# Five engine queues of a hybrid decoder step: orders by the scheduler and a partial table, replaced by whole tables

## The chip, the cores and the metric

The kernel runs on one core of a Trainium2 chip. The metric is the device time of one execution in microseconds (us). The kernel before took 2063.24 us (median of 3 runs, 2061.25 to 2066.89). A core has five engines, each with a queue of instructions that it works through in order: TensorE (PE, matrix products; PEld is its weight loading), VectorE (DVE), ScalarE (ACT), GpSimd (POOL) and SyncE (SP, which here issues most of the DMA transfers). Engines wait for each other through semaphores. The order in which a queue holds its instructions is fixed when the program is built.

## The reference, cut to what matters

One layer of a hybrid decoder for a prompt of 2048 tokens and 8 single decode tokens, in fp32, with a model width of 1024:

```python
xn = _rmsnorm(x, norm1_g)
z = jnp.einsum('btd,de->bte', xn, w_in)            # 1792 columns: RG-LRU x | gate | q | k | v
xr, gr, q, k, v = jnp.split(z, IN_SPLITS, axis=-1)
xc, new_conv = _causal_conv(xr, conv_buf, conv_w, conv_b)
hs, h_last = _rglru(xc, h0, ...)                    # gated linear recurrence over the tokens
rec = hs * jax.nn.gelu(gr)
att, ... = sliding-window attention (8 heads of 64, 2 KV heads, window 128, a sink per head)
mix = jnp.concatenate([_rmsnorm(rec, rec_norm_g), _rmsnorm(att, attn_norm_g)], axis=-1)
h = x + jnp.einsum('bte,ed->btd', mix, w_out)
hn = _rmsnorm(h, norm2_g)
ff = jax.nn.silu(hn @ w_gate) * (hn @ w_up)         # 2816 wide
y = h + ff @ w_down
```

Then a final RMSNorm. The outputs are y, the last 128 K and V rows, the conv history and the recurrent state, for prompt and decode tokens.

## The kernel before, in words

**Products.** Each fp32 matrix is split into a high and a low part, and each product is made of three matmuls (high by high, high by low, low by high), so that one 128x128 block of weights over 8 blocks of the contraction takes 24 matmuls.

**First half (up to about 690 us).** The 2056 tokens are cut into four sub-blocks (s = 0 to 3, 520 + 3 x 512). For each, the input projection makes 14 column units (products ip{s}_{u}); the units feed conv, gates (products g{s}_{c}) and scan of the recurrent branch on VectorE and ScalarE (`rec_chunk`, `gate_chunk`), and attention items of 128 queries and one KV head (`attn_item`): scores s, a softmax, transposes pt, their copies to SBUF as high part `pth` (ScalarE, L984) and low part `ptl` (VectorE, L985), products o with V, and the addition into `ratt` (L997). Group norms (`group_norm`, with small products st_ for sums and bc_ for broadcasting; rc is the recurrent group, at the attention group) lead to the output projection (products op{s}_{m}; `out_unit`, and `out_half` for the last sub-block), whose result is added to the residual `xres` and stored to `hs` in device memory.

**Second half.** The feed-forward part works on three token groups gi = 0, 1, 2 of two halves each (344 or 342 columns) and 11 pairs p of weight blocks. Gate and up products of a pair are done by a seven-product scheme for 2x2 blocks (keys g{gi}_{p}_{r} and u{gi}_{p}_{r}; `products`). It needs mixed inputs: `hn_mix` loads rows of `hs` (tiles n, L517; scaled on VectorE, L521; added, L529) and stores sums to `mixed`; `hn_load` loads them and splits them into hn. Weight sums are made from loads rg, ru and rd on ScalarE, VectorE and GpSimd (L1224, L1225, L1259, L1294, L1326). VectorE adds the products from PSUM into c_g and c_u (L1410); ScalarE copies some (L1431 to L1438) and applies SiLU (L1389). The down projection runs on the high and low parts fh, fl (L1380, L1381) either plainly (`down`, products pd, VectorE adds into y at L1469) or in the seven-product way (`down_parts`, products pw, adds at L1500). The final norm of the last group is `finish_last`: f21 is the second half of group 2, which ends first, and f20 the first half; each has sums (st_f), a root and a reciprocal (L1558, L1559), a broadcast product (bc_f), eight scalings (L1577; for f20 two on GpSimd, L1575) and eight stores.

**What sets the order.** Each step of work is a generator that is handed to `Chains`, which runs generators by time and sets a priority for the scheduler that then makes each engine's queue. `at` and `ahead` move the priority of single instructions. On top stand hand-made orders, as dependencies that hold two instructions of one engine in order and need no semaphore: `PE_ORDER`, a table of TensorE's products by key and count from the start into the first pair of the feed-forward part; `AFTER`, seven pairs on VectorE and ScalarE; `FIRST_DVE` for the first sub-block's splits; `keep`, which holds some loads and products in program order; and, for the end, `F_PLACE`, `F_HOLD` with the lists `tail_pd`, `tail_add`, `ends`, `held`. The rest, TensorE's order from then on included, is the scheduler's.

**Fillings.** `filled` puts matmuls of a block of ones into a PSUM tile before its first real product, as many as `FILLS` counts under the key w_ and the tile's name:

```python
for _ in range(FILLS["w_" + name]):
```

There are 75 of them, each 128x256: 17 before the first sums (w_st_x0), 13 before w_st_at0, 13 before w_op3_0_0, 20 in eight small groups (5 w_g1_2_0_0, 4 w_pt2_0_0, 4 w_ps_u0_0_2, 2 w_pt15_0_0, 2 w_op3_3_1, one each of w_bc_x1_0, w_o8_0, w_bc_rc3_0), and at the end 9 w_st_f2_0 and 3 w_bc_f2_0.

Of the kernel before, what the change touches and what calls it, by code (L numbers as in the profile page):

```python
# [59 lines left out]
F_PLACE = [3, 6]  # L60
F_HOLD = [2, 5]
# [19 lines left out]
def plan():  # L81
# [34 lines left out]
ip0_1_1:3 ip0_12_0 ip0_1_0:2 ip0_1_1:2 ip0_12_0 ip0_1_0 ip0_1_1 ip0_12_0:4 ip0_12_1:6 ip0_1_0:3 ip0_1_1:3 ip0_12_0:3
ip0_1_0:2 ip0_1_1:2 ip0_12_0:2 ip0_12_1:5 ip0_9_0:5 st_x0:5 ip0_9_0:9 ip0_9_1:24 ip0_9_0:10 bc_x0_0:4 ip0_8_0:24
ip0_8_1:4 bc_x0_4 ip0_8_1:20 ip0_0_0:24 ip0_0_1:23 g0_1_0_0 ip0_0_1 ip0_3_0:24 g0_1_0_260 ip0_3_1:17 g0_1_1_0
ip0_3_1:7 ip0_11_0:18 g0_1_1_260 ip0_11_0:6 ip0_11_1:15 vt0_0 ip0_11_1:9 ip0_10_0:23 vt0_1 ip0_10_0 ip0_10_1:24
ip0_13_0:10 vt0_2 ip0_13_0:14 ip0_13_1:6 vt0_3 ip0_13_1:18 ip0_2_0:7 s0_0_0:4 ip0_2_0:5 g0_0_0_0 s0_0_1:4 ip0_2_0:12  # L120
ip0_2_1:6 s0_1_0:4 s0_1_1:4 ip0_2_1:2 g0_0_0_260 ip0_2_1:13 pt0_0_1:4 ip0_2_1 s1_0_0:4 ip0_2_1:2 ip0_5_0:3 s1_0_1:4
ip0_5_0 g0_0_1_0 ip0_5_0:9 o0_0_0 ip0_5_0:11 ip0_5_1 s1_1_0:4 ip0_5_1:2 pt0_1_1:4 o0_0_0 ip0_5_1:4 g0_0_1_260
ip0_5_1:12 s1_1_1:2 o0_1_0 s1_1_1:2 ip0_5_1:5 ip0_4_0:6 s2_0_0:4 ip0_4_0:3 o0_1_0 ip0_4_0:11 pt1_0_0:4 ip0_4_0:2
s2_0_1:4 ip0_4_0:2 ip0_4_1:24 ip1_8_0:15 ip0_6_0:2 o1_0_0 ip0_6_0:8 pt1_0_1 o1_0_0 pt1_0_1:3 ip0_6_0 ip1_8_0
g0_3_0_0 ip0_6_0:13 ip0_6_1 ip1_8_0:2 ip0_6_1:15 o1_0_1 g0_3_0_260 s2_1_0:4 ip0_6_1 ip1_8_0 ip0_6_1 pt1_1_0
ip0_6_1:5 o1_0_1 s2_1_1:4 pt1_1_0:3 ip0_6_1 ip1_8_0:5 ip1_9_0 g0_3_1_0 ip1_9_0:19 ip0_7_0:9 ip1_9_0:2 pt1_1_1 o1_1_0
pt1_1_1:3 g0_3_1_260 ip1_9_0:2 ip0_7_0:2 o1_1_0 ip0_7_0:13 w_bc_x1_0 bc_x1_0 s3_0_0:3 s3_0_1:4 ip0_7_1 s3_0_0
ip0_7_1 o1_1_1:2 bc_x1_0 w_pt2_0_0:4 ip0_7_1 bc_x1_0 ip0_7_1 bc_x1_0 ip0_7_1:2 pt2_0_0:4 ip0_7_1:18 ip1_10_0:2
o2_0_0:2 pt2_0_1:3 g0_2_0_0 ip1_10_0:12 pt2_0_1 ip1_10_0:10 ip1_11_0:2 o2_0_1 ip1_11_0 s3_1_0:4 pt2_1_0:4 g0_2_0_260
ip1_11_0 s3_1_1:4 ip1_11_0:2 o2_0_1 ip1_11_0:11 g0_2_1_0 pt2_1_1:3 ip1_11_0:7 ip1_4_0:4 o2_1_0 ip1_4_0 pt2_1_1  # L130
ip1_4_0 o2_1_0 g0_2_1_260 ip1_4_0:18 ip1_0_0:2 o2_1_1 ip1_0_0 vt1_0 ip1_0_0:6 dS:2 o2_1_1 pt3_0_0:4 ip1_0_0:5 dS:6
ip1_0_0:6 o3_0_0 ip1_0_0:4 ip1_12_0:2 dS2:2 ip1_12_0:2 pt3_0_1 o3_0_0 ip1_12_0:2 pt3_0_1:3 ip1_12_0:18 ip1_13_0:6
o3_0_1 ip1_13_0:2 o3_0_1 ip1_13_0:3 pt3_1_0:4 ip1_13_0:9 dS3 ip1_13_0 dS3 ip1_13_0:3 ip1_1_0:8 pt3_1_1:2 o3_1_0
pt3_1_1 ip1_1_0:2 pt3_1_1 o3_1_0 dS4:4 s4_0_0 ip1_1_0:2 o3_1_1 s4_0_1:3 s4_0_0:3 s4_0_1 dS4:4 ip1_1_0 o3_1_1
ip1_1_0:11 ip1_5_0:6 dS5:2 s4_1_0:2 s4_1_1:4 ip1_5_0 vt1_1 ip1_5_0:3 s4_1_0:2 ip1_5_0:8 pt4_0_0:2 ip1_5_0 pt4_0_0:2
ip1_5_0:5 ip1_2_0:2 s5_0_0:4 ip1_2_0 s5_0_1:4 ip1_2_0 vt1_2 ip1_2_0:8 o4_0_0 ip1_2_0:6 pt4_0_1 o4_0_0 pt4_0_1:3
ip1_2_0:3 vt1_3 ip1_2_0:3 o4_0_1 s5_1_0:4 s5_1_1:4 o4_0_1 st_rc0 pt4_1_0:4 st_rc0:4 ip1_6_0:15 pt4_1_1:4 bc_rc0_0:3
s6_0_0:4 bc_rc0_0 s6_0_1 ip1_6_0:4 s6_0_1:3 pt5_0_0 bc_rc0_4 pt5_0_0:3 g1_0_0_0 g1_0_1_0 w_st_at0:13 ip1_6_0
st_at0:5 ip1_6_0:4 ip1_3_0:24 ip1_7_0:3 bc_at0_0:4 ip1_7_0:18 bc_at0_4 ip1_7_0:3 op0_0_0:12 op0_0_260:8 g1_1_0_0
op0_0_260:4 op0_1_0:12 op0_0_0 op0_0_260 op0_1_0 op0_0_260:2 op0_0_0:3 op0_1_0:6 op0_0_0:6 op0_1_0:3 op0_0_260:9  # L140
g1_1_1_0 op0_0_0:2 op0_1_0:2 o4_1_0:2 op0_1_260:4 o4_1_1:2 op0_1_260:20 op0_2_0:11 pt5_0_1:4 o5_0_0:2 op0_2_0:13
op0_2_260:13 s6_1_0:3 s6_1_1:4 s6_1_0 op0_2_260:4 o5_0_1 op0_2_260:7 op0_3_0 w_g1_2_0_0:5 g1_2_0_0 pt5_1_0
op0_3_0:12 o5_0_1 op0_3_0:2 pt5_1_0:3 op0_3_0:9 op0_3_260:17 g1_2_1_0 op0_3_260:7 op0_4_0:24 op0_4_260:6 pt5_1_1:4
op0_4_260:2 o5_1_0:2 op0_4_260:16 op0_5_0 o5_1_1 op0_5_0:11 s7_0_0:4 op0_5_0:3 o5_1_1 op0_5_0:4 s7_0_1:4 pt6_0_0:2
# [24 lines left out]
ip3_4_0:2 ip3_1_0:2 g3_0_0_0 ip3_1_0:2 s13_0_0 pt12_0_0 o11_1_1 pt12_0_0 ip3_1_0 pt12_0_0:2 ip3_1_0:5 s13_0_0:3
# [1560 lines left out]
```

## Time and profile before

| | |
|---|---|
| median of 3 runs | 2063.24 us (2061.25 to 2066.89) |
| profiled execution, first to last instruction | 2054.6 us |
| median of the runs less that span | 8.6 us |
| TensorE busy | 2015.9 us (98%) |
| weight loading busy | 1908.1 us (93%) |
| VectorE busy | 1459.9 us (71%) |
| ScalarE busy | 944.6 us (46%) |
| GpSimd busy | 906.5 us (44%) |
| granted TensorE clock, mean | 0.997 |

The span is that of one execution taken by the hardware profiler; its own time outside the span is not recorded, so its distance to the median of the runs stands in the table. In rows of groups, the columns are: source line, engine, operation, output and inputs by tile names, shape, count; busy time and mean duration in ns; idle time of the engine just before, and what ended it. In rows of windows: stretch, length, busy time and count of PE, PEld, DVE, ACT and POOL, granted clock (1.00 is full), DMA share and GB/s. In rows of a timeline: start, duration, engine, line, operation, tiles, shapes, count, and in brackets the idle time before with its releaser. In rows of waits: engine, operation and line that waited, what ended the wait; sum, times, longest, in us.

### The profile page before, as it was taken

Reading aid. Unit: us, or ns where it says so; the run is one execution under the profiler, and the core shown is the slowest. Engines: PE = TensorE matmul, PEld = TensorE weight load, DVE = VectorE, ACT = ScalarE, POOL = GpSimd, SP = SyncE. Lnnn points to the kernel's source line nnn. Section 1 sums busy time; section 2 is a strip of 40 time slices with the busy share of each in tenths; the row PEclk is TensorE's granted clock in tenths of the full one; section 3 lists DMA queues with packets and bytes.
Section 4 is the critical chain, followed back from the end, with each engine's and each line's share of the span. In section 5 each row is a group of like instructions: output and inputs, shape, how many; then the busy total and the mean of one; then the engine's idle time right before and its main releaser. Section 6 shows DMA issues by size and latency. Waiting matters only on the chain.

```text
span 2054.6 us, 34857 instructions
## 1 busy us (share of the span) xinstructions
PE 2015.9 (98%) x12319; PEld 1908.1 (93%) x12319; DVE 1459.9 (71%) x2694; ACT 944.6 (46%) x1960; POOL 906.5 (44%) x799
## 2 busy tenths in 40 slices
PE   9999999999999999999999999999999999999998
PEld 9988787878777899999999999999999999999998
DVE  6877886767985766666654667777768666777675
ACT  6764774553664543343334533333335433433343
POOL 5311342020122787567656645556457522322333
PEclk9999999999999999999999999999999999999999
DMA  9864584576688856666546677776677675566652
GB/s 329 293 213 143 188 275 159 175 233 210 208 261 280 314 200 223 205 210 207 207 172 210 229 260 258 227 229 221 222 253 265 211 251 189 183 197 196 197 179 96
DMA packets 208991, 450.98 MB, mean 219 GB/s; under 512 B 25232, under 2 KB 82720, under 8 KB 208800
## 3 DMA queue, kind: packets, MB, share of 16 engines
q1 hardware_dynamic: 205184, 445.73, 65.2%
q10 hardware_dynamic: 3632, 3.02, 0.4%
q8 instruction: 97, 1.59, 0.3%
q14 instruction: 78, 0.64, 0.1%
HBM read 335.89 MB, written 113.84 MB: 219 GB/s over the span
## 4 chain that ended last, share of the span: by engine, by line
PE 77%; DVE 9%; DMA 6%; ACT 3%; issue 2%; POOL 1%; SPq 0%; DVEq 0%; ACTq 0%; POOLq 0%
PE ps_u L396 19%; PE ps_g L396 19%; PE pw L396 11%; PE pd L396 10%; PE ip L396 10%; PE op L396 4%; DMA n<-hs 3%; DMA xs<-in_xT 1%; DMA m<-mixed 1%; PE o L396 1%; PE pt L401 1%; DVE sc L974 1%; DVE sc L963 1%; PE s L396 1%; DMA mixed<-n 1%
## 5 line engine op out<-in xcount | busy, mean ns | idle before, releaser
L396 PE MATMUL ps_g<-hn,w_g 128*128 128x342 f32 (+1 forms) x2772 | 489.4, 320 | 4.6 <-DVE c_u L1410 1.8
L396 PE MATMUL ps_u<-hn,w_u 128*128 128x342 f32 (+1 forms) x2772 | 479.9, 319 | 1.9 <-ACT c_u L1436 1.3
L396 PEld LDWEIGHTS ps_g<-hn,w_g 128*128 128x128 f32 x2772 | 445.1, 188 | 6.0 <-DVE c_u L1410 2.3
L396 PEld LDWEIGHTS ps_u<-hn,w_u 128*128 128x128 f32 x2772 | 444.2, 188 | 2.6 <-ACT c_u L1436 1.6
L396 PE MATMUL ip<-xn,w_in 128*128 128x512 f32 (+1 forms) x1680 | 353.4, 358 | 1.9 <-ACT xn L431 1.8
L396 PEld LDWEIGHTS ip<-xn,w_in 128*128 128x128 f32 x1680 | 270.1, 189 | 46.0 <-issue 3.8
L1500 DVE TENSOR_TENSOR y<-y,pw 128x342 f32<-128x342 f32 x504 | 238.7, 504 | 73.0 <-PE pw L396 72.2
L396 PE MATMUL pd<-fh,w_d 128*128 128x344 f32 (+1 forms) x960 | 239.4, 320 | 0.6 <-DVE y L1469 0.6
L396 PE MATMUL op<-mix,w_out 128*128 128x512 f32 (+1 forms) x960 | 203.4, 357 | 0.5 <-DVE rrec L763 0.3
L396 PEld LDWEIGHTS op<-mix,w_out 128*128 128x128 f32 x960 | 155.4, 188 | 29.3 <-issue 5.0
L1469 DVE TENSOR_TENSOR y<-y,pd 128x344 f32<-128x344 f32 (+1 forms) x240 | 117.9, 507 | 75.3 <-PE pd L396 70.7
L396 PEld LDWEIGHTS pd<-fh,w_d 128*128 128x128 f32 x960 | 168.3, 188 | 1.4 <-DVE y L1469 1.1
L396 PE MATMUL pw<-fh,wd 128*128 128x342 f32 x576 | 165.6, 319 | 1.2 <-DVE y L1500 1.2
L396 PE MATMUL pd<-fl,w_d 128*128 128x344 f32 (+1 forms) x480 | 153.4, 320 | 0.0
L1381 DVE TENSOR_TENSOR fl<-c_u,fh 128x342 fp32r<-128x342 f32 (+1 forms) x132 | 107.1, 815 | 48.3 <-ACT fh L1380 47.9
L1225 POOL TENSOR_TENSOR w_u<-ru,w_u 128x512 fp32r<-128x512 f32 x44 | 58.9, 1338 | 181.6 <-ACT w_u L1224 155.0
L1392 POOL TENSOR_TENSOR c_u<-c_u,c_g 128x342 f32<-128x342 f32 (+1 forms) x60 | 60.5, 1008 | 170.7 <-DVE c_u L1410 132.1
L1380 ACT CAST fh<-c_u 128x342 fp32r<-128x342 f32 (+1 forms) x132 | 63.0, 480 | 157.8 <-POOL c_u L1392 61.9
L396 PE MATMUL pw<-t,wd 128*128 128x342 f32 x648 | 126.7, 320 | 2.6 <-DVE t L1381 1.7
L1410 DVE TENSOR_TENSOR c_u<-c_u,ps_u 128x342 f32<-128x342 f32 (+1 forms) x99 | 50.2, 507 | 100.3 <-PE ps_u L396 100.1
L396 PEld LDWEIGHTS pw<-t,wd 128*128 128x128 f32 x648 | 106.0, 188 | 4.4 <-DVE t L1381 2.5
L396 PEld LDWEIGHTS pw<-fh,wd 128*128 128x128 f32 x576 | 105.3, 189 | 1.7 <-DVE y L1500 1.5
(316 smaller groups left out, 3507.4 us busy)
## 6 DMA issues: line engine op xcount, KB each, us to landing
w_g<-split_g SPq DMA_DIRECT2D x88, 512.0 KB, 4.2
w_u<-split_u SPq DMA_DIRECT2D x88, 512.0 KB, 4.9
w_in<-split_w SPq DMA_DIRECT2D x84, 512.0 KB, 3.5
rg<-in_wgate SPq DMA_DIRECT2D x110, 256.0 KB, 3.1
ru<-in_wup SPq DMA_DIRECT2D x110, 256.0 KB, 3.2
w_out<-split_w SPq DMA_DIRECT2D x48, 512.0 KB, 4.4
split_g<-w_g SPq DMA_DIRECT2D x44, 512.0 KB, 3.6
split_u<-w_u SPq DMA_DIRECT2D x44, 512.0 KB, 2.7
```

The lines of the kernel that those rows point to most:

```text
L396: r = nc.tensor.matmul(*args, **kw)
L401: r = nc.tensor.transpose(*args)
L963: seen[f"sm{gb}_{kv}_{g}"] = nc.vector.tensor_tensor_reduce(sc[:, g, :kn], ps[:, gi * 256:gi * 256 + kn], mask[:, k0:k0 + kn], -SCALE, ns[ ...
L974: nc.vector.tensor_scalar(sc[:, g, :kn], sc[:, g, :kn], mx[:, 1, g:g + 1], None, ALU.mult)
L1225: lo_eng.tensor_tensor(w[:, 1, :], src, w[:, 0, :].bitcast(F32), op=ALU.subtract)
L1380: nc.scalar.copy(hi, v)
L1381: nc.vector.tensor_tensor(lo, v, hi.bitcast(F32), ALU.subtract)
L1392: (nc.vector if p == NPAIR - 1 or src is not v else eng(E_MUL[2 * h + n])).tensor_tensor(v, src, g, op=ALU.mult)
L1410: nc.vector.tensor_tensor(o, a, b, op)
L1469: r = nc.vector.tensor_tensor(ys[gi, n, m], ys[gi, n, m], ps, ALU.add)
L1500: nc.vector.tensor_tensor(v, v, ps, ALU.add)
```

## The change

The orders of all five queues are now stated for the whole program, in a table `ORDER` with one text for each engine. An entry is a key, for ":n" instructions in a row, with "+k" taking the k-th of those that the key has left instead of the first. TensorE's keys are products as before; the other engines' keys are the generators, whose instructions `Chains` now records. `order` chains each queue by the same semaphore-free dependencies as before, and takes every instruction that a key has. `PE_ORDER`, `AFTER`, `FIRST_DVE`, `keep`, `F_PLACE`, `F_HOLD` and the lists of the tail are removed, and so are the fillings that the tables don't have: 46 of 75 go, 17 w_st_x0, 9 w_st_f2_0 and 3 w_bc_f2_0 stay. Tiles, buffers, transfers and arithmetic are as before, and so are the counts of instructions on the four other engines.

```diff
-AFTER = [
-    ("xl2_5", "xc1_2_3"), ("xt3_1", "pth5_1_1"),
...
-PE_ORDER = """
-w_st_x0:13 ip0_1_0 ip0_1_1 w_st_x0:4 ip0_12_0 ip0_12_1 ip0_1_0:2 ip0_1_1:2 ip0_12_0:2 ip0_12_1:2 ip0_1_0 ip0_1_1
...
-s6_0_0:4 bc_rc0_0 s6_0_1 ip1_6_0:4 s6_0_1:3 pt5_0_0 bc_rc0_4 pt5_0_0:3 g1_0_0_0 g1_0_1_0 w_st_at0:13 ip1_6_0
-st_at0:5 ip1_6_0:4 ip1_3_0:24 ip1_7_0:3 bc_at0_0:4 ip1_7_0:18 bc_at0_4 ip1_7_0:3 op0_0_0:12 op0_0_260:8 g1_1_0_0
...
-op0_3_0:12 o5_0_1 op0_3_0:2 pt5_1_0:3 op0_3_0:9 op0_3_260:17 g1_2_1_0 op0_3_260:7 op0_4_0:24 op0_4_260:6 pt5_1_1:4
-op0_4_260:2 o5_1_0:2 op0_4_260:16 op0_5_0 o5_1_1 op0_5_0:11 s7_0_0:4 op0_5_0:3 o5_1_1 op0_5_0:4 s7_0_1:4 pt6_0_0:2
...
+ORDER = {
+    "PE": """
+w_st_x0:17 ip0_1_0 ip0_1_1 ip0_12_1 ip0_12_0 ip0_1_0:2 ip0_1_1:2 ip0_1_0 ip0_12_1 ip0_1_1 ip0_12_0:2 ip0_12_1 ip0_12_0
...
+s5_1_1:4 pt4_1_1:4 bc_rc0_0:4 ip1_5_0:2 o4_0_1 ip1_5_0 bc_rc0_4 o4_0_1 ip1_5_0 s6_0_0 ip1_5_0 g1_0_0_0 ip1_5_0
+ip1_6_0:11 g1_0_1_0 ip1_6_0:6 s6_0_0:3 ip1_6_0:2 s6_0_1:3 pt5_0_0 ip1_6_0:3 st_at0 ip1_6_0 st_at0 ip1_6_0 st_at0
+ip1_3_0 st_at0 ip1_3_0 st_at0 ip1_3_0:22 ip1_7_0:2 bc_at0_0:3 s6_0_1 bc_at0_0 ip1_7_0:6 pt5_0_0 bc_at0_4 ip1_7_0:16
...
+d2_10_6_1:6 d2_10_7_1:6 d2_10_0_0:6 d2_10_1_0:6 d2_10_2_0:6 d2_10_3_0:2 st_f2_1:3 d2_10_3_0:4 d2_10_4_0:6 d2_10_5_0:6
+d2_10_6_0:6 bc_f2_1 d2_10_7_0:6 w_st_f2_0 bc_f2_1 w_st_f2_0:2 bc_f2_1 w_st_f2_0:6 w_bc_f2_0:3 st_f2_0:6 bc_f2_0:3
+""",
+    "DVE": """
...
+f00 wg1.1 pu1.0 f00 pu1.0 mix2+1 pu1.0 pu1.0+1 pu1.0+1 pu1.0:3 f01 pu1.0 pg1.1 mix2:2 f00 mix2 mix2+2 mix2 pg1.1 f01+2
...
+pu2.10 d2.9+1 pu2.10:2 pu2.10+1 pu2.10+1 d2.9 pu2.10:3 d2.9:2 pu2.10 d2.10:3 f21 d2.10:2 f21 d2.10:2 f21 d2.10:2 f21
+d2.10:4 f21 d2.10:3 f21:8 f20:7
+""",
...
-    def add(self, gen):
+    def add(self, name, gen):
+        self.names[gen] = name
         self._advance(gen, 0.0)
+
+    def record(self, name, first):
+        for i in self.traced[first:]:
+            self.made.setdefault((ENGINES.get(i.engine), name), []).append(i)
...
-        def behind(later, earlier):
-            tc.add_manual_dep(later.ins, earlier.ins.name, no_sync, reason="issue order")
...
+        def order(runs, todo):
+            last = None
+            for run in runs.split():
+                key, _, at = run.partition("+")
+                key, _, n = key.partition(":")
+                for _ in range(int(n or 1)):
+                    r = todo[key].pop(int(at or 0))
+                    if last is not None:
+                        tc.add_manual_dep(r, last.name, no_sync, reason="issue order")
+                    last = r
+            assert not any(todo.values()), [k for k, v in todo.items() if v]
 
         def order_engines():
...
+            order(ORDER["PE"], {k: [r.ins for r in v] for k, v in issued.items()})
+            for e in ORDER:
+                if e != "PE":
+                    order(ORDER[e], {k: list(v) for (x, k), v in ch.made.items() if x == e})
...
-            for place, r in zip(F_PLACE, ends):
-                for m in range(place, KD):
-                    behind(tail_pd[m], r)
-            for i, r in enumerate(held):
-                if i >= F_HOLD[0]:
-                    behind(r, eps_op[0] if i >= F_HOLD[1] else tail_add[0])
...
-            order_pe()
             order_engines()
```

In the table of VectorE the names are: pg and pu the adds of gate and up products of group.pair, d those of the down projection, wg, wu and wd the weight sums, mix1 and mix2 the mixing of groups 1 and 2, f00 to f21 the final norms, o35b the second half of column block 5 of the last output projection, hl0 the later part of group 0's hn.

More of the change, by code (lines that the diff above doesn't have):

```diff
@@ L116 @@
[L116 to L120, printed above, removed]
@@ L231 @@
 NV = 73
+ENGINES = {mybir.EngineType.DVE: "DVE", mybir.EngineType.Activation: "ACT", mybir.EngineType.Pool: "POOL",
+           mybir.EngineType.SP: "SP"}
 class Chains:
@@ L248, in _advance @@
         self.tc.cur_priority = int(now * 100)
+        first = len(self.traced)
         try:
@@ L252, in _advance @@
             return
+        finally:
+            self.record(self.names[gen], first)
         t, keys = (r[0], r[1:]) if isinstance(r, tuple) else (r, ())
@@ L1462, in down @@
                         hi, lo = ts[gi, p, (h, n)]
-                        r = mm(f"d{gi}_{p}_{m}_{n}", ps, w[:, 0, c:c + P], hi, start=h == 0, stop=False)
-                        if last and gi == 2 and not h and not n:
-                            tail_pd[m] = r
+                        mm(f"d{gi}_{p}_{m}_{n}", ps, w[:, 0, c:c + P], hi, start=h == 0, stop=False)
                         mm(f"d{gi}_{p}_{m}_{n}", ps, w[:, 0, c:c + P], lo, start=False, stop=False)
```

930 lines of the change are left out of this document (723 added, 207 removed).

## The prediction

> **What bounds the kernel now.** I read first the busy times, then the span cut at the kernel's stages, then what TensorE waited for, then short timelines.
>
> ```profile
> span 2054.6 us, 34857 instructions
> PE 2015.9 (98%) x12319; PEld 1908.1 (93%) x12319; DVE 1459.9 (71%) x2694; ACT 944.6 (46%) x1960; POOL 906.5 (44%) x799
> ```
>
> TensorE idles 2054.6 − 2015.9 = 38.7 us. No product is dropped by the change and no operand altered, so an order can win back idle time and filling products only. By stages (columns: stretch, length, busy time of each engine, granted clock, DMA share, GB/s):
>
> ```profile
> 0.00:60.00 60.00, 56.35 (x435) 55.26 (x436) 42.06 (x85) 36.53 (x73) 32.66 (x38) 1.00 0.92 330
> 60.00:200.00 140.00, 138.54 (x849) 120.98 (x848) 110.08 (x285) 92.78 (x222) 28.52 (x39) 1.00 0.63 213
> 200.00:216.00 16.00, 12.83 (x69) 10.06 (x68) 13.00 (x30) 10.45 (x23) 0.85 (x3) 0.89 0.11 34
> 216.00:290.00 74.00, 69.32 (x470) 61.29 (x469) 63.54 (x110) 55.43 (x111) 35.94 (x31) 1.00 0.80 264
> 290.00:640.00 350.00, 345.00 (x1702) 279.91 (x1701) 265.69 (x555) 188.46 (x389) 70.04 (x81) 1.00 0.65 211
> 640.00:720.00 80.00, 75.65 (x413) 67.75 (x412) 53.20 (x72) 38.77 (x78) 46.90 (x33) 1.00 0.89 315
> 720.00:1080.00 360.00, 360.00 (x2292) 360.00 (x2291) 233.93 (x349) 140.98 (x279) 242.47 (x181) 1.00 0.59 203
> 1080.00:1240.00 160.00, 158.68 (x1025) 158.29 (x1024) 95.23 (x162) 69.26 (x149) 95.47 (x84) 1.00 0.68 232
> 1240.00:1480.00 240.00, 234.44 (x1476) 231.45 (x1475) 181.50 (x312) 87.70 (x178) 137.33 (x124) 1.00 0.71 231
> 1480.00:2040.00 560.00, 559.43 (x3567) 558.09 (x3566) 393.74 (x723) 221.59 (x456) 211.73 (x185) 1.00 0.63 203
> 2040.00:2054.60 14.60, 5.63 (x42) 5.04 (x40) 7.96 (x17) 2.67 (x6) 4.63 (x6) 0.75 0.56 193
> ```
>
> Length less the first busy figure is TensorE's idle time: 3.65 at the start, 1.46, 3.17, 4.68, 5.00, 4.35, then 0, 1.32, 5.56, 0.57, and 8.97 in the tail. Between start and tail that is 26.1 us; the 360 us from 720 and nearly all of 1480 to 2040 have nothing to give. What ended the idle time (sum, times, longest):
>
> ```profile
> PE pt L401 <- DVE ptl L985: 3.1, 6, 1.1
> PE o L396 <- ACT pth L984: 2.9, 2, 2.1
> PE pw L396 <- DVE y L1500: 2.0, 3, 1.2
> PE ps_g L396 <- DVE c_u L1410: 1.8, 2, 0.9
> PE ps_g L396 <- DVE c_g L1410: 1.8, 1, 1.8
> PE pw L396 <- DVE t L1381: 1.7, 3, 1.1
> PE ps_u L396 <- DVE c_g L1410: 1.6, 2, 1.0
> PE ps_u L396 <- ACT c_u L1436: 1.3, 1, 1.3
> PE ps_g L396 <- DVE xres L1135: 1.0, 1, 1.0
> ```
>
> These are many waits of 2.1 us or less, all on VectorE or ScalarE working in their queue's order, none on a weight's transfer. Such a wait goes when its producer stands earlier or its consumer later, which is what whole-queue tables can do.
>
> **The change, part by part.** On VectorE, ScalarE, GpSimd and SyncE it adds and removes nothing; it moves instructions (on VectorE 2090 of 2566, mostly by a few places). The order-only dependencies take no semaphore. On TensorE 46 of the 75 fillings go: 13 st_at, 15 op, and 18 in small groups.
>
> ```profile
> L396 PE MATMUL op<-ones 128*128 128x256 f32 x15 | 2.2, 287 | 0.0
> 208.48 1.13 PE L396 MATMUL g<-xc,gw 128*128 128x512 f32 x2 [0.78 <-ACT ra L802]
> 210.60 0.68 ACT L802 ACTIVATE ia<-g,hxb 128x512 f32<-128x512 f32 x1
> 211.33 3.09 PE L396 MATMUL st_at<-ones 128*128 128x256 f32 x13 [1.73 <-ACT ia L802]
> 206.00:211.00 5.00, 2.62 (x8) 0.72 (x6) 4.91 (x9) 3.79 (x8) 0.00 (x0) 0.98 0.00 0
> 211.00:214.00 3.00, 2.67 (x12) 2.67 (x13) 3.00 (x6) 2.99 (x6) 0.00 (x0) 0.50 0.00 0
> ```
>
> Fillings: op 2.2 us / 15 = 0.147 us each; the 18 others at that price 2.6; st_at 3.1. Together 7.9 us, at most: a removed filling gains only where its successor was ready.
>
> *200 to 216.* The old order uses up the ip1_6 products first and then has only the two gate products, a wait for ia, and 13 fillings, at a granted clock of 0.50. The table keeps ip1_5, ip1_6 and ip1_3 products back and puts them between bc_rc0, s6, the gate products and st_at0. So idle 3.17 + fillings 3.1 = 6.3 us can go. Cover: about 25 input-projection products. VectorE is 4.91 of 5.00 busy there, so attention behind it may still be late: 0 to −6.3, I take −5, since here the work that fills the hole is named.
>
> *60 to 200*: idle 1.46 plus five small fillings 0.7 = 2.2; −1.
>
> *216 to 290.* The largest wait is o5_1_1, for pth behind pt5_1_1:
>
> ```profile
> 268.92 2.21 PE L396 MATMUL op<-mix,w_out 128*128 128x260 f32 x17
> 272.60 0.57 ACT L984 CAST pth<-pt 128x512 fp32r<-128x512 f32 x1
> 273.22 0.50 PE L396 MATMUL o<-pth,vt 128*128 128x512 f32 x1 [2.09 <-ACT pth L984]
> ```
>
> An op product takes 2.21 / 17 = 0.13 us. The table puts pt5_1_1 18 products later (2.3 us), and the second half of o5_1_1 15 products further from it (2.0 us); on VectorE and ScalarE gate and conv work goes behind ptl and pth. That covers the two waits of 2.1 and 1.1 us. VectorE is busy 63.54 of 74 us, so of idle 4.68 plus five fillings 0.7 I take a bit over half: −3; bounds −5.4 and +1 (one such wait left elsewhere).
>
> *290 to 640*: the same attention pattern, idle 5.00, and 17 fillings (13 op, four small) at 2.5, in a stage where VectorE is busy 265.69 of 350. 7.5 at most; half, −4; bounds 0 and −7.5.
>
> *640 to 720.* The first pair's evacuations stand behind adds of the output projection and weight work:
>
> ```profile
> 695.47 0.50 DVE L1410 TENSOR_TENSOR c_g<-c_g,ps_g 128x344 f32<-128x344 f32 x1
> 696.12 0.40 PE L396 MATMUL ps_g<-hn,w_g 128*128 128x344 f32 x1 [1.78 <-DVE c_g L1410]
> ```
>
> The table moves o35b's adds, hl0 and w_g/w_u preparations behind them. DMA is at 0.89 here, so what is moved back (hn, weights) may be late next. Idle 4.35 plus six fillings 0.9; −3; bounds +2 (the wait above goes to w_g) and −5.2.
>
> *1080 to 1240*: c_u on ScalarE (1.3 us) gets hn1 work behind it: −1.
>
> *1240 to 1480.* The waits on L1500, L1381 and L1410, 5.56 us of idle time. The work of mix2 (loads n, rows L521 and L529) is pulled forward about 70 us:
>
> ```profile
> L521 DVE SCALAR_TENSOR_TENSOR n<-n,vec,hb 128x342 f32<-128x342 f32 x14 | 9.8, 703 | 26.1 <-DMA n<-hs 26.1
> DVE n L521 <- DMA n<-hs: 51.5, 29, 4.7
> 1165.00:1240.00 75.00, 75.00 (x491) 74.99 (x490) 46.18 (x83) 24.72 (x52) 36.00 (x34) 1.00 0.73 241
> ```
>
> VectorE stands still for these loads, 26.1 us in 14 of them, with its evacuations queued behind. The later half is relieved; 1165 to 1240, at present full, takes the load: VectorE has 75 − 46.18 = 28.8 us free there. I take −2.5; bounds −5.6 and +10 (see the rivals).
>
> *Start*: 17 fillings in one row where 4 stood apart, and the first product waits for xn anyway: 0.
>
> *Tail.* The old order lets two of f21's eight scalings pass before the last adds and three before f20's reciprocal. The table puts all eight between the last add and that reciprocal.
>
> ```profile
> 2041.85 0.51 DVE L1469 TENSOR_TENSOR y<-y,pd 128x342 f32<-128x342 f32 x1 [0.42 <-PE pd L396]
> 2042.28 1.53 DVE L1577 SCALAR_TENSOR_TENSOR y<-y,vec,bc_f 128x342 f32<-128x342 f32 x3
> 2044.84 0.18 DVE L1559 RECIPROCAL cols_f<-cols_f 114x3 f32<-114x3 f32 x1 [1.03 <-ACT cols_f L1558]
> 2046.56 2.98 DVE L1577 SCALAR_TENSOR_TENSOR y<-y,vec,bc_f 128x342 f32<-128x342 f32 x6
> ```
>
> From 2041.85 + 0.51 = 2042.36, eight at 1.53 / 3 = 0.51 end at 2046.44 instead of the reciprocal's start at 2044.84: f20's scalings and the last outputs come 1.6 us later. The adds before them come up to 1 us earlier, but output transfers may bunch: +0.5 to +2.5, I take +1.6.
>
> Sum: −1 − 5 − 3 − 4 − 3 − 1 − 2.5 + 1.6 = −17.9, so a span of 2036.7. The median of the runs, 2063.24, lies 8.6 above the span shown; with that, **2045 us**.
>
> **The rivals.**
>
> A, the forecast: about half of idle time and fillings goes; own range 2036 to 2054.
>
> B, nearly all of it: 26.1 + 7.9 − 1.6 = 32.4, giving 2031. For it: no wait is longer than 2.1 us, and TensorE has product streams to put anywhere. Against: VectorE at 80 to 86% in 60 to 290 leaves little room, and every producer moved up moves another back.
>
> C, the waits only change place: the hole at 200 goes (−5), small waits come back elsewhere, the tail costs 1.6; with a little of the fillings, −4: 2059 (2052 to 2067). For it: the stages that lose are those where VectorE is fullest. Against: where VectorE is at 65% (720 on), there is no wait at all, so slack exists to be borrowed.
>
> D, the clock falls without the fillings. The row 206 to 211 shows that a stretch with TensorE busy 2.62 of 5.00 us was followed by 3 us at clock 0.50, which costs 1.5 us of work. If each of the five places of four or more removed fillings (st_at0, pt2, g1_2, op3_0_0, ps_u0) did that, 7.5 us come back: 2053. Against: four of the five lie in stages at 1.00 whose single waits are short. [...]
>
> E, slower: the loads n of mix1 and mix2, 32 instructions pulled forward on the in-order VectorE queue, into evacuations that are on time now. Each stop of VectorE for a load (51.5 / 29 = 1.8 us) that meets a full set of accumulators costs TensorE about the largest wait on y, 1.2 us. From 15 such hits (15 × 1.2 = 18) the forecast gain is eaten; at 24 it is +29 − 18 = +11: 2074. For it: 26.1 us of such stops stand in the same stretch as most of the waits of 1240 to 1480. Against: from 720 to 1080 mix1 runs through with no idle time.
>
> **How the numbers follow.** Chances: A 0.52, B 0.10, C 0.20, D 0.05, E 0.13. 0.3% is 6.2 us, about what a measurement tells from no change. Faster by more than that (under 2057): all of A, B, D and a quarter of C, 0.72. Slower (over 2069.4): most of E and a little of C, 0.13. The rest 0.15. Range 2031 to 2068: it leaves out E's bulk and half of B, under 2 in 10.
>
> **What would show it.** Right: 200 to 216 with no fillings and clock 1.00; idle time near 2 us each in 216 to 290, 290 to 640 and 640 to 720; no 2 us wait on pth; f20's reciprocal about 4.1 us after the last add; the end about 1.6 us later after it than now. Wrong: new rows of TensorE waiting on y or c_u between 750 and 1430 (E), the same sums under other names before 720 (C), a clock below 1.00 after 20 us (D), or DMA as releaser of TensorE.

## The result

The changed kernel takes 2035.98 us (median of 4 runs, 2033.65 to 2039.23) where the kernel before, beside it, takes 2062.24 us (2060.93 to 2066.89): a ratio of 0.9869, 95% interval 0.9853 to 0.9884, so about 26 us or 1.3% less. The forecast was 2045 (range 2031 to 2068). The profiled execution has a span of 2033.4 us and took 2035.2. One execution of the kernel before, among the 25 beside e1 to e4, took 3295.19 us at a granted clock of 0.556; it is left out of the ratios.

The page's first part, and the windows of the same bounds as before (the last two end where the new tail begins):

```profile
span 2033.4 us, 34750 instructions
PE 2004.7 (99%) x12273; PEld 1904.5 (94%) x12273; DVE 1472.9 (72%) x2694; ACT 955.0 (47%) x1960; POOL 906.8 (45%) x799
```

```profile
0.00:60.00 60.00, 55.09 (x419) 53.92 (x420) 38.63 (x82) 35.38 (x71) 29.64 (x36) 0.97 0.93 334
60.00:200.00 140.00, 140.00 (x872) 123.26 (x871) 117.95 (x298) 99.11 (x235) 30.03 (x42) 1.00 0.63 208
200.00:216.00 16.00, 16.00 (x85) 13.09 (x84) 14.81 (x25) 10.12 (x19) 4.58 (x5) 1.00 0.50 163
216.00:290.00 74.00, 73.52 (x526) 67.33 (x525) 71.51 (x125) 59.64 (x114) 36.85 (x31) 1.00 0.80 269
290.00:640.00 350.00, 344.67 (x1652) 277.84 (x1651) 268.29 (x548) 189.62 (x390) 69.87 (x80) 0.99 0.67 218
640.00:720.00 80.00, 76.35 (x443) 72.05 (x442) 54.20 (x78) 39.11 (x79) 54.56 (x39) 0.98 0.85 303
720.00:1080.00 360.00, 360.00 (x2289) 359.75 (x2289) 235.37 (x341) 146.19 (x283) 245.83 (x182) 1.00 0.58 202
1080.00:1240.00 160.00, 157.37 (x1015) 156.56 (x1014) 113.72 (x181) 65.96 (x142) 90.93 (x79) 1.00 0.76 257
1240.00:1480.00 240.00, 239.62 (x1525) 239.32 (x1524) 181.00 (x315) 90.52 (x181) 142.05 (x130) 1.00 0.70 231
1480.00:2020.00 540.00, 538.96 (x3442) 538.65 (x3442) 370.54 (x693) 218.01 (x445) 199.98 (x178) 1.00 0.59 198
2020.00:2033.40 13.40, 3.08 (x26) 2.71 (x24) 6.85 (x15) 1.33 (x4) 2.52 (x3) 0.71 0.61 210
```

TensorE's idle time (length less its busy time) was 1.46, 3.17 and 4.68 us from 60 to 290 and is 0, 0 and 0.48. It was 5.56 from 1240 to 1480 and is 0.38. But from 290 to 640 it is 5.33 (5.00 before), from 640 to 720 3.65 (4.35), at the start 4.91 (3.65). So two stretches were emptied, and two kept what they had under other names, as the waits show:

```profile
PE pt L968 <- DVE ptl L1537: 4.4, 4, 2.1
PE ps_u L963 <- ACT c_u L1985: 3.5, 1, 3.5
PE ip L963 <- ACT w_in L936: 2.7, 3, 1.6
PE bc_f L963 <- DVE cols_f L2103: 1.8, 1, 1.8
```

The waits on ia, y at L1500 and t are gone, and of those on ra (2.0 us) 0.2 is left. One wait on ptl of 2.1 us, one on c_u of 3.5 us and one in the tail of 1.8 us are new.

Since both kernels hold the same products, each can be found again in both traces. The table gives the start of the last product of a kind in the profile of before, and how much earlier (negative) it starts in the others. "e" numbers are the experiments below.

```
              before   after    e1     e5     e3     e10    e6
ip0            125.0    -0.9   -0.0   +0.5   +1.2   +0.4   +0.4
ip1            228.4    -8.9   -1.3   -7.4   -0.1   -7.6   -7.6
op0            298.7   -15.8   -1.3  -13.5   -0.7  -14.4  -14.7
op2            620.1   -16.9   -1.4  -12.7   -2.6  -13.3  -16.7
u, group 0.0   713.0   -16.4   +1.2  -11.0   -1.8  -12.4  -20.9
d, group 0.10 1150.3   -16.0   +2.2  -11.5   -1.5  -11.9  -20.3
u, group 1.3  1299.2   -14.6   +2.7   -7.2   -0.3  -11.1  -18.5
u, group 1.7  1464.9   -21.4   +4.2   -7.8   -7.2   -9.9  -26.0
d, group 2.10 2041.5   -22.8   +3.8   -6.7   -9.9  -11.9  -27.6
bc_f2_0       2045.6   -21.1   +4.1   -6.7   -8.2  -10.2  -27.1
```

The column of after is a staircase with two steps: 15 us between 125 and 299, and 7 us between 1299 and 1465. Between them nothing is won, and the tail gives 1.7 back. A second execution of the changed kernel (e7) has the same two steps: −0.8 to −15.4 and −11.9 to −18.6.

Of the 21.2 us between the two spans, 10.0 are TensorE's idle time (38.7 to 28.7) and 11.2 its busy time (2015.9 to 2004.7). The dropped fillings held it busy for 7.7 us in the trace of before; where the other 3.5 us of busy time went is not shown.

### The profile page after: what moved, and what is told of

Its sections match the earlier page's. It is cut to its first block, busy times and chain, and to the rows that moved or that the text cites. A ratio compares the mean times of both kernels' runs of the same rounds, so it can differ in the third digit from the quotient of the medians.

```text
span 2033.4 us, 34750 instructions
## 1 busy us (share of the span) xinstructions
PE 2004.7 (99%) x12273; PEld 1904.5 (94%) x12273; DVE 1472.9 (72%) x2694; ACT 955.0 (47%) x1960; POOL 906.8 (45%) x799
## 4 chain that ended last, share of the span: by engine, by line
PE 88%; DMA 6%; DVE 4%; issue 1%; ACT 1%; SPq 0%; DVEq 0%; ACTq 0%
PE ps_g L963 20%; PE ps_u L963 20%; PE ip L963 14%; PE pw L963 12%; PE pd L963 11%; PE op L963 5%; PE s L963 1%; DMA m<-mixed 1%; PE g L963 1%; PE pt L968 1%; PE o L963 1%; DMA mixed<-n 1%; DMA y<-hs 1%; DMA xs<-in_xT 0%; DMA hn<-mixed 0%
## 5 line engine op out<-in xcount | busy, mean ns | idle before, releaser
L963 PE MATMUL ps_g<-hn,w_g 128*128 128x342 f32 (+1 forms) x2772 | 546.0, 320 | 1.8 <-DMA w_g<-split_g 1.0
L963 PE MATMUL ps_u<-hn,w_u 128*128 128x342 f32 (+1 forms) x2772 | 529.8, 320 | 4.5 <-ACT c_u L1985 3.5
L963 PEld LDWEIGHTS ps_u<-hn,w_u 128*128 128x128 f32 x2772 | 455.0, 189 | 5.5 <-ACT c_u L1985 3.8
L963 PEld LDWEIGHTS ps_g<-hn,w_g 128*128 128x128 f32 x2772 | 456.6, 189 | 2.5 <-ACT w_d L1778 2.3
L963 PE MATMUL ip<-xn,w_in 128*128 128x512 f32 (+1 forms) x1680 | 367.3, 361 | 3.9 <-ACT w_in L936 2.7
L963 PE MATMUL op<-mix,w_out 128*128 128x512 f32 (+1 forms) x960 | 209.8, 362 | 0.3 <-DVE mix L999 0.3
L963 PE MATMUL pw<-t,wd 128*128 128x342 f32 x648 | 150.6, 319 | 0.0
L963 PE MATMUL pd<-fl,w_d 128*128 128x344 f32 (+1 forms) x480 | 147.6, 320 | 0.0
L1935 DVE TENSOR_TENSOR fl<-c_u,fh 128x342 fp32r<-128x342 f32 (+1 forms) x132 | 118.5, 909 | 15.3 <-ACT fh L1934 14.2
L963 PEld LDWEIGHTS pw<-t,wd 128*128 128x128 f32 x648 | 111.4, 189 | 0.0
```

Of the source, the lines that this page charges most:

```text
L963: r = nc.tensor.matmul(*args, **kw)
L1935: nc.vector.tensor_tensor(lo, v, hi.bitcast(F32), ALU.subtract)
```

## The experiments

All kernels use the form of the changed kernel: a table for each queue. Ratios and times are to the kernel before, run on the same chip beside them.

**e1: the old orders, written as tables.** All five queues in the order of the kernel before, with its 75 fillings.

```diff
 ORDER = {
     "PE": """
-...   (the new tables)
+...   (the five old queues, entry by entry)
```

> The kernel before, its five queues written out as tables in the new form, all 75 fillings kept. Theory (only the order counts; and the profiled execution of before, 2054.6 us, was a quick one, because after the change the time of a run is its span plus 1.8 us): the same time as before within 3 us, and a span about 1.8 us less than the run's own time, so 2057 to 2064, with more idle time of TensorE than 38.7 us somewhere. Rival (a fixed 8.6 us lies around the span of before, as the prediction's sum took it): span 2054 to 2056 in a run of 2062 to 2064.

2060.79 against 2061.10 us, ratio 1.000 (0.999 to 1.0009). The profiled execution took 2060.57 and has a span of 2058.8: 1.8 us apart, as in the changed kernel (2035.2 and 2033.4). So writing tables does nothing by itself, only the order counts, and the 8.6 us of the prediction's sum were not a fixed surround: the profiled execution of before was a quick one. The column e1 above shows the size of such differences between two executions of one order: up to 1.4 us to 620, about 4 at the end.

**e2: new orders to the end of the first output projection, then old.**

```diff
-...   (new tables)
+...   (new tables for what started before 283 us; the rest in the old order)
```

> New orders on all engines for what started before 283 us in the new profile (to the end of the first output projection), the old orders from there. Theory (the gain lies in two places: 16 us between 125 and 299 us, 6 us between 1330 and 1440, and nothing net between): 14 to 18 us faster than before, the old waits of 1240 to 1480 back. Rival (the gain is spread, as the prediction had it: 9 of 19.5 us up to 290): 9 to 11 us faster.

2057.52 against 2061.10 us, ratio 0.9988 (0.9975 to 1.0001). Both expectations missed: at the end of op0 the kernel is 14.5 us ahead of the profile of before, and one stage later (ip2) only 4.0. From there to ip2 it loses 10.5 us to the kernel before. The longest wait of that stretch is more than half of it:

```profile
PE st_h L823 <- POOL hacc L870: 5.8, 1, 5.8
```

The sum hacc waits for a square on ScalarE. At the seam that square stands behind six items of a later sub-block's input, which wait for transfers (3.5, 2.4 and 2.2 us), and four exponentials of an attention item: work that the new orders had put off and that the old order of ScalarE takes first. Another 3.7 us are longer products: TensorE is busy 98.27 us between op0 and ip2, and 94.60 in the kernel before, with a granted clock of 0.97 against 1.00. This cannot tell a real gain from a borrowed one, hence e5.

**e5: the same with the seam at the end of the last output projection** (663 us in the new profile).

> New orders on all engines for what started before 663 us in the new profile (to the end of the last output projection), old orders from there; the seam stands where TensorE is nearly always fed. Theory (the 16 us up to 299 are a real gain of the new orders; e2 lost 10 of them again because its old orders met work that the new ones had put off): 13 to 18 us faster than before, and 15 us or more ahead of the control e1 at the first pair. Rival (the early gain is borrowed, and what was put off comes due wherever the new orders end): 3 to 8 us faster, 8 us or more given back within 100 us of the seam.

2045.08 against 2058.47 us, ratio 0.9941 (0.9920 to 0.9963), 13.4 us. The 13.5 us at op0 are still 11.0 at the first pair, 12.2 ahead of the control e1 (+1.2 there); less than the 15 expected. The rival, a gain that is only borrowed, falls: from op2 to the first pair 1.7 us are given back, and not 8.

**e3: old orders to the end of op0, new from there.**

> The other way round: old orders for what started before 298.7 us in the profile of before, new ones from there. Theory: 4 to 7 us faster than before, with the new waits at 594 to 612 and 676 in it and the tail 1.6 us longer. Rival (spread gain): 10 us or more.

2051.18 against 2061.10 us, ratio 0.9948 (0.9932 to 0.9965): 9.9 us, above the 4 to 7 expected, at the rival's edge. But the gain is not spread: the column e3 is at −2.6 at op2, back at −0.3 at 1299, and then falls to −9.9. Its largest waits, 5.7 us on ptl in 6 and 5.1 on c_u in one, stand at the places of the changed kernel's. The 13.4 us of e5 and these 9.9 add up to 23.3, between the 21.4 (e7) and 26 us of the whole change.

**e4: the old orders without the 46 fillings.**

```diff
-...  g1_0_0_0 g1_0_1_0 w_st_at0:13 ip1_6_0 ...
+...  g1_0_0_0 g1_0_1_0 ip1_6_0 ...
```

(so for the other nine groups, in the old table of TensorE)

> The old orders without the 46 fillings that the change drops. Theory of the prediction (a filling counts only where its successor is ready; 7.9 us at most): 2 to 5 us faster than before, because the sums behind the 13 at half clock are then the next to be waited for. Rival (the clock falls without them): 0 to 7 us slower, granted clock below 0.99 in more than one stretch. Second rival (they all counted): 7 to 8 us faster.

2059.29 against 2061.10 us, ratio 0.999 (0.9979 to 1.0001): 1.8 us, at the lower edge of what the first theory gave and not clear of nothing. In the trace of before the 46 fillings hold TensorE busy for 7.7 us, in e1's, which has the same order, for 6.8. Yet TensorE is as busy without them, in e1 and in e4:

```profile
PE 2018.4 (98%) x12319; PEld 1908.7 (93%) x12319; DVE 1458.9 (71%) x2694; ACT 944.3 (46%) x1960; POOL 907.3 (44%) x799
```

```profile
PE 2018.7 (98%) x12273; PEld 1909.0 (93%) x12273; DVE 1457.0 (71%) x2694; ACT 944.6 (46%) x1960; POOL 907.3 (44%) x799
```

Their 6.8 us went into real products that took longer, for the granted clock falls in several stretches. One of them, in e4 and in the kernel before:

```profile
630.00:640.00 10.00, 10.00 (x37) 8.18 (x36) 5.26 (x11) 2.31 (x5) 1.02 (x1) 0.72 0.30 84
```

```profile
630.00:640.00 10.00, 10.00 (x50) 8.24 (x49) 6.92 (x14) 2.68 (x6) 1.02 (x1) 1.00 0.60 176
```

0.72 where it was 1.00. Between 30 us and the tail the clock is at 0.50 for 20.5 us in e4 (from 212, 629, 700 and 1250 us), for 6.8 in e1 (from 622 and 697) and for 3.4 in the kernel before (from 211). So in the old orders the fillings cost little and bought clock; dropping them alone is not the gain.

**e8: TensorE's table alone.** The other queues are left to the scheduler.

```diff
             order(ORDER["PE"], {k: [r.ins for r in v] for k, v in issued.items()})
-            for e in ORDER:
-                if e != "PE":
-                    order(ORDER[e], {k: list(v) for (x, k), v in ch.made.items() if x == e})
```

> TensorE's table of the change alone; the four other queues are left to the scheduler, without the pairs and lists that were removed. Theory (the gain is TensorE's consumers placed later and fillings dropped, with the producers' order second): 8 to 14 us faster than before. Rival (the producers' order is what counts, the tables are one whole): within 4 us of before, or slower, with waits on ptl, ra and y longer than 2 us.

2097.89 against 2058.47 us, ratio 1.0198 (1.0178 to 1.0217): 39 us slower. My theory, that consumers placed later carry the gain, fell. Its longest waits:

```profile
PE o L963 <- DVE ratt L1546: 5.0, 1, 5.0
PE o L963 <- ACT pth L1533: 4.9, 3, 3.6
PE ip L963 <- ACT xn L995: 4.7, 1, 4.7
```

**e11: the four other tables alone**, TensorE by the scheduler.

```diff
-            order(ORDER["PE"], {k: [r.ins for r in v] for k, v in issued.items()})
             for e in ORDER:
```

> The four tables of VectorE, ScalarE, GpSimd and SyncE alone; TensorE's order is left to the scheduler (its fillings are those of the new table). After e8, where TensorE's table alone was 40 us slower: theory (the tables are one whole; each queue's order is right only with the others): 5 to 50 us slower than before. Rival (the producers' tables carry the gain): 10 us or more faster than before.

2073.84 against 2062.35 us, ratio 1.0053 (1.0033 to 1.0073): 11.5 us slower. Either half alone, with the scheduler's order for the rest, is worse than the old mixture. That the tables are one whole fits this, but two things stand beside it. Both kernels also lack the old hand-made orders of the other half; the new table of TensorE with the old order of the other queues, or the reverse, was not run. And both lack the 46 fillings: the granted clock is at 0.50 between 12 us and the tail for 41 us in e8 and 44 us in e11, where e1 has 6.8. TensorE's idle time is 26.9 us above e1's in e8 (67.3 against 40.4) but only 7.0 in e11 (47.4); the rest of the loss lies in longer products.

**e10: mix2 put back.** Only the instructions of mix2, on every engine, stand again between their old neighbours.

```diff
-f00 wg1.1 pu1.0 f00 pu1.0 mix2+1 pu1.0 pu1.0+1 pu1.0+1 pu1.0:3 f01 pu1.0 pg1.1 mix2:2 f00 mix2 mix2+2 mix2 pg1.1 f01+2
+...  (the same without mix2, whose 16 loads and their work follow some 70 us later)
```

> The changed kernel with mix2's instructions alone, on every engine, put back between the neighbours that they had in the old orders (some 70 us later). Theory (it is mix2's loads stopping VectorE among the waited sums that cost the 5.5 us between 1330 and 1440, and starting earlier took that away): 3 to 6 us slower than the changed kernel, 2039 to 2042, waits on y, t and c_u back between 1300 and 1480. Rival (the order of the other work there did it): within 2 us of 2036.

2046.93 against 2062.35 us, ratio 0.9923 (0.9896 to 0.9950); the changed kernel's is 0.9869 beside its own runs of before and 0.9898 in e7, so about 5 to 11 us are lost, rather more than the 3 to 6 expected, and the rival (within 2 us) falls. From 1299 to 1465 the changed kernel wins 6.8 us, this one loses 1.2; that makes 8.0, and the rest of its distance was there before mix2 began. VectorE's loads from 1080 to 1500 in the kernel before, here, and in the changed kernel (up to 1480, when all 16 are done); the last two figures are its idle time before them:

```profile
L521 DVE SCALAR_TENSOR_TENSOR n<-n,vec,hb 128x342 f32<-128x342 f32 x16 | 11.2, 706 | 29.3 <-DMA n<-hs 29.3
```

```profile
L1082 DVE SCALAR_TENSOR_TENSOR n<-n,vec,hb 128x342 f32<-128x342 f32 x16 | 10.7, 672 | 35.1 <-DMA n<-hs 34.6 <-DVE fl L1935 0.4
```

```profile
L1082 DVE SCALAR_TENSOR_TENSOR n<-n,vec,hb 128x342 f32<-128x342 f32 x16 | 15.7, 1010 | 0.0
```

VectorE stood still 29.3 us for these loads before, 34.6 with mix2 late, and not at all in the changed kernel. And TensorE's waits from 1240 to 1480 in e10 are on y again, 5.1 us where the kernel before has 2.0 (those on t and c_u did not come back):

```profile
PE pw L963 <- DVE y L2050: 5.1, 4, 2.1
PE pw L963 <- DVE fl L1935: 0.8, 1, 0.8
```

From the end of a load's issue on SyncE to the VectorE instruction that reads it there are 4.5 us (median of the 16 loads) in the kernel before, 4.6 in e10 and 16.6 in the changed kernel. The short distance, the stops and the loss come and go together. But e10 moves the loads, their readers and the stores at once, so it does not part the distance from the place: no run changed the order on SyncE against VectorE alone.

**e7: the changed kernel again.**

> The changed kernel again, beside the others. Both theories: 2034 to 2038, ratio to before 0.985 to 0.989; its profile shows which waits are the same in two executions: I expect those at 594 to 612, 676 and in the tail to be, each within 1 us.

2037.06 against 2058.47 us, ratio 0.9898 (0.9880 to 0.9917), its upper end a little above what was expected. The waits come at the same places: ptl 4.6 us in 4, c_u 3.3, the tail's 1.8.

**e6: three moves in the changed kernel.** Each takes the cause of a new wait from ahead of it on its queue.

```diff
 DVE, tail
-f21 d2.10:3 f21:8 f20:7
+f21 d2.10:3 f21:5 f20 f21:3 f20:6
 DVE at 666
-o37b hl0 wu0.0 pg0.0 o35b:2 hl0
+o37b o35b:2 wu0.0 pg0.0 hl0:2
 ACT at 668 (o35b is its store to hs)
-wu0.0 hl0 pg0.0+1 wu0.0 pg0.0+1 pg0.0 o35b hl0
+wu0.0 o35b hl0 pg0.0+1 wu0.0 pg0.0+1 pg0.0 hl0
 DVE at 591 and 608 (a321, a331: ptl copies)
-o25 mix0:3 a321
+o25 a321 mix0:3
-rn3+1 rn3+2 hn0 a331
+rn3+1 a331 rn3+2 hn0
```

> The new orders with three moves. Tail: the reciprocal of f20 behind five of f21's eight scalings. At 676: the adds of o35b on VectorE and its store on ScalarE's queue before the work of hl0, w_u and the table load. At 594 and 609: two ptl copies before mix0's and rn3's work on VectorE. Theory (each wait has the in-order cause read in the profile): the reciprocal 1.2 us earlier after the last add, the 3.5 us wait on c_u below 1, the two waits on ptl of 2.1 and 1.2 us gone; 5 to 7 us faster than the changed kernel, 2029 to 2031. Rival (DMA, busy all through 668 to 684, and later links set the end): 1 to 3 us faster, the wait on c_u still over 2.

2029.19 us beside 2037.06 for the changed kernel in e7 on the same chip: 7.9 us less, ratio to before 0.9857 (0.9841 to 0.9873) against 0.9898. The wait on c_u, 3.5 us in the changed kernel, is in e6:

```profile
PE ps_u L963 <- ACT c_u L1985: 0.2, 1, 0.2
```

What it came from stands in ScalarE's timeline of the changed kernel:

```profile
671.88 1.28 ACT L1943 ACT_TABLE_LOAD   x1
673.18 0.49 ACT L1943 ACTIVATE c_g<-c_g 128x344 f32<-128x344 f32 x1
673.86 0.35 ACTq L1688 DMA_DIRECT2D hs<-xres  x1
679.96 0.45 ACT L1985 COPY c_u<-ps_u 128x344 f32<-128x344 f32 x1 [4.18 <-DMA m<-mixed]
```

The last store of xres was issued behind a table load and a SiLU, and the copy into c_u, which in the program waits for four transfers, came 6.1 us after it. With the store at 670.42 the wait is gone. The trace names a load of m as the last transfer to land; which of the four was late is not shown singly, and with the store o35b's adds and one step of hl0 were moved too. The tail's part is plain in VectorE's rows, of the changed kernel and of e6:

```profile
2019.06 0.51 DVE L2021 TENSOR_TENSOR y<-y,pd 128x342 f32<-128x342 f32 x1 [0.66 <-PE pd L963]
2019.85 3.94 DVE L2119 SCALAR_TENSOR_TENSOR y<-y,vec,bc_f 128x342 f32<-128x342 f32 x8 [0.28 <-PE bc_f L963]
2023.70 0.17 DVE L2103 RECIPROCAL cols_f<-cols_f 114x3 f32<-114x3 f32 x1
```

```profile
2014.27 0.51 DVE L2021 TENSOR_TENSOR y<-y,pd 128x342 f32<-128x342 f32 x1 [0.66 <-PE pd L963]
2015.06 2.50 DVE L2119 SCALAR_TENSOR_TENSOR y<-y,vec,bc_f 128x342 f32<-128x342 f32 x5 [0.28 <-PE bc_f L963]
2017.69 0.17 DVE L2103 RECIPROCAL cols_f<-cols_f 114x3 f32<-114x3 f32 x1
```

From the end of the last add to the reciprocal 4.13 us (2023.70 − 2019.57) against 2.91, and from that add to the end 13.8 (2033.4 − 2019.57) against 12.4 (2027.2 − 2014.78).

**e12: e6 without the two ptl moves.**

> The kernel of e6 without the two ptl moves (tail and o35b only). Theory (the ptl waits at 594 and 609 went, but op3 then waited for the mix of rn3, so they were not what set the end there; of e6's 7.9 us, 6 are o35b's and 1.4 the tail's): 2029 to 2031, as e6. Rival (each wait removed counts): 2 to 4 us slower than e6.

2028.99 us, ratio 0.9832 (0.9810 to 0.9854): as e6. The ptl waits are back (1.9 and 1.2 us), and the last product of op3 comes as early as with the moves (15.5 us ahead of before, e6 15.2). So the longest wait in a list need not be the one that sets the end of its stage: op3 comes no earlier when it goes.

**e9: fillings put back at one place**, in e6.

```diff
-o15_0_1 pt15_1_0:4 o15_0_1 st_h2:4 pt15_1_1:2 op3_0_0
+o15_0_1 w_op3_0_0:8 pt15_1_0:4 o15_0_1 st_h2:4 w_op3_0_0:8 pt15_1_1:2 op3_0_0
```

> The kernel of e6 with 16 fillings of ones put back on op3_0_0's tile, 8 before pt15_1_0 and 8 before the last transposes pt15_1_1. In e6 TensorE has short work from 605 to 611 (0.61 us busy of 606 to 608) and the granted clock is then 0.50 to 0.81 to 620. Theory (the old 13 fillings here kept the clock, rival D at one of its five places): clock 1.00 from 606 to 620, 1 to 3 us faster than e6, 2026 to 2028. Rival (the waits there set the time, and a filling takes 0.12 us of it): same as e6 or up to 2 us slower.

The clock is as the first theory said. Windows of the changed kernel (where e6 has 0.50 to 0.81 as well) and of e9:

```profile
606.00:608.00 2.00, 1.08 (x6) 0.61 (x6) 2.00 (x3) 0.99 (x2) 1.24 (x1) 1.00 1.00 278
608.00:610.00 2.00, 1.14 (x9) 0.97 (x8) 2.00 (x4) 1.25 (x3) 0.03 (x1) 0.78 0.65 241
610.00:612.00 2.00, 1.67 (x7) 1.31 (x7) 1.97 (x5) 1.96 (x4) 1.52 (x1) 0.50 0.36 104
614.00:616.00 2.00, 2.00 (x7) 1.52 (x6) 2.00 (x4) 0.00 (x0) 0.00 (x0) 0.51 0.97 320
```

```profile
606.00:608.00 2.00, 1.74 (x14) 1.40 (x12) 2.00 (x3) 0.99 (x2) 1.23 (x1) 1.00 1.01 278
608.00:610.00 2.00, 2.00 (x17) 1.91 (x17) 1.94 (x4) 1.97 (x4) 0.04 (x1) 1.00 0.70 255
610.00:612.00 2.00, 2.00 (x13) 1.61 (x12) 2.00 (x5) 1.82 (x4) 1.40 (x1) 1.00 0.22 43
614.00:616.00 2.00, 2.00 (x10) 1.62 (x9) 1.74 (x3) 0.20 (x1) 0.00 (x0) 1.00 0.70 192
```

In its profile the last product of op3 is 18.8 us ahead of before, against 15.5 in e12. But that execution, 2023.48 us, was the quickest of four, and the median is 2028.41 us, ratio 0.9826 (0.9802 to 0.9850), not to be told from e12's 0.9832. So the clock is shown, and the 3 us are not. In the changed kernel the clock was halved at 609 us, in a stretch of 4 us (606 to 610) in which TensorE was busy 2.2 (1.08 and 1.14).

e6, e9 and e12 beat both kernels: by 1.4 to 1.7% of before, and e6 by 0.4% of the changed kernel beside it.

## Why the prediction was right, point by point

The direction and the range held; the time was 9 us too high. The span was forecast at 2036.7 and is 2033.4, so 3.3 of the 9 us are the sum, and the rest is **the step from span to median**: 8.6 us by the prediction, 2.6 measured. Of these 2.6, 1.8 lie between span and time of one execution, in e1 and in the changed kernel, and 0.8 between the profiled execution and the median. The two times that the prediction compared were of different executions, and the profiled one was quick. That is the term that was most mis-sized. That the sum itself is off by only 3.3 is in part luck: two stages before 290 us and the one from 1240 gave 2 to 4.3 us more than forecast, three others 2.8 to 3.5 us less.

- *60 to 216*: −6 forecast, −8.0 between the ends of ip0 and ip1. Mechanism as told: no fillings, clock 1.00, no idle time. The cover was better than assumed; the attention producers behind a full VectorE did not come late. No run put a single move of this stretch or the next back, so which move earned what is read from the traces and not tested.
- *Start*: 0 forecast. Idle time rose by 1.3 us with new waits on w_in, and 0.9 was won by the end of ip0.
- *216 to 290*: −3 forecast, −6.9 measured (ends of ip1 and op0), past the bound of −5.4. The share "a bit over half" was too low: idle time between these two products fell from 4.68 to 0.48. The other 2.7 us are busy time, of which five dropped fillings explain 0.6; the rest is open. VectorE went from 63.5 to 71.5 us busy of 74: being nearly full did not stop it from serving in time.
- *290 to 640*: −4 forecast, about −1 measured (−15.8 at op0, −16.9 at op2). The step that failed is the price of the fillings. I counted half of idle time plus fillings; by e4 the fillings, in the old orders, were worth 1.8 us all together, and here the idle time stayed (5.33), with the clock halved from 609 to 616. Rival D thus came true at one of its five places, op3_0_0.
- *640 to 720*: −3 forecast, +0.5 measured. The prediction had said that what is moved back may be late next and put it at w_g. It was the copy into c_u, 3.5 us, probably behind the store of xres, and e6 took it away. Behind that wait the clock was at 0.50 from 681 to 684, near another of D's places (ps_u0); whether its four fillings would have held it was not tried.
- *1080 to 1240*: −1 forecast; idle time rose from 1.32 to 2.63 us, and by the table 1.8 us are lost from 713 to 1299. The largest of the new waits, 1.0 us at 1199 (1.5 in e7), is on y, where VectorE stood for a load `y<-hs`: rival E's mechanism with another load.
- *1240 to 1480*: −2.5 forecast, −6.8 measured, past the bound of −5.6 (from 1299 on, to within what two executions differ). The prediction saw that mix2 was relieved there but feared the earlier stretch (rival E). It looked at VectorE's free time and not at how long a load is issued ahead of its reader. With 16.6 us instead of 4.5 the stops for mix2's loads are 0.0 us where they were 29.3: E's mechanism was real, and here the change removed it. Over the whole program VectorE's stops for loads n fell from 51.5 to 4.8 us; those for loads of y rose from 3.7 to 9.4.
- *Tail*: +1.6 forecast, +1.6 measured (from the last add to the end 13.8 us, before 12.24 from 2042.36 to 2054.6), with the reciprocal 4.13 us after the add where 4.1 was forecast.
- *Fillings as 7.9 us at most*: they were 7.7 in the trace of before. In the old orders their removal left idle time as it was (40.2 us in e4, 40.4 in e1), and what they had taken went into longer products, with the clock at 0.50 for 20.5 us in e4 and 6.8 in e1. The prediction named a filling without a ready successor as the way to gain nothing; it was the clock, its rival D.

Of the rivals, C (waits that change place) held from 290 to 720, and on a small scale from 1080 to 1240; B did not come about, though e12 and e6 at 2029 show that it was within reach.

Of the signs that the prediction named for being right, four came: 200 to 216 without fillings at clock 1.00, no 2 us wait on pth, the reciprocal 4.1 us after the last add, the end 1.6 us later after it. Idle time near 2 us in each of three stages did not: 0.48, 5.33 and 3.65. Of the signs for being wrong, all four showed to some extent: the same sums under other names before 720, the clock at 0.50 from 609 and 681, one new wait on y (1.0 us), and transfers as releaser of TensorE (1.0 us for w_g, 0.8 for w_u). So the mechanism of the forecast held from 60 to 290 us and from 1240 to 1480, and not in the stages between.

Open: why e3 gains 9.9 us where the step of 7 and a loss in the tail would give 5 to 6, and what the quick executions of before did better; the differences build up in many places of less than 2 us.

## What to carry to other kernels

When a whole queue is reordered, look at the time between a load's issue and its reader on the in-order engine (here 4.5 us with 29.3 us of stops, 16.6 us with none), and not only at how busy that engine is; here VectorE's own waits had 51.5 us of stops for loads n, where TensorE's list had 2.0 us on y. Orders of several queues must be judged together: half of a good set, with the scheduler's order for the rest, was 39 or 11 us worse than the mixture it replaced. A filling that looks like waste may hold the clock (from 630 to 640 us it was 1.00 in the kernel before and 0.72 in e4): count what the products behind it gain. And before a span is carried over to a median, ask for the time of that very execution.

## What was not expected of the hardware

- The same order, run again, moves by up to 4 us within one execution's profile and from 2059.37 to 2063.33 us in ten runs (e1), with its differences in waits of at most about 2 us. Two rows that the prediction used are among them: the wait of 2.1 us on pth before 290 us is at most 0.3 in e1's trace, and the clock of 0.50 at 211 us is 1.00 there.
- The granted clock fell behind stretches in which TensorE still had work: it was 0.57 from 598 to 602 in e7 behind 1.49 us of work in 4, and 0.50 from 609 in the changed kernel behind 2.58 us of work in 4 (605 to 609). No share of load that decides it can be read off: in the changed kernel, 1.89 us of work in the 4 us from 594 left it at 1.00.
